# A hybrid decoder layer on one core: seven products for eight in some chunk pairs of the feed-forward streams, and eight PSUM banks as two alternating sets

## The chip, the cores and the metric

One core of a Trainium2 chip runs the whole layer. The metric is device time in microseconds (us) of one execution; lower is better. Before the change the median of three runs is 1110.67 us (1109.77 to 1110.89).

## The reference

The input is a sequence of 256 tokens by 2048 features, float32. After a normalisation and a combined input projection, two groups of attention heads run (latent attention and differential attention); their outputs are concatenated and go through one output projection `w_o`, which is added to the input. What the change touches is the feed-forward part behind it:

```
h = rmsnorm(x, ffn_norm)
x = x + (silu(h @ w_gate) * (h @ w_up)) @ w_down
```

`w_gate` and `w_up` are 2048 x 5632, `w_down` is 5632 x 2048. All of it is float32, and the result is compared as such.

## The kernel before, in words

**Streams.** Every projection is a *stream* (`stream`, L111): a weight matrix of up to 1024 columns is read from memory in order and used once, against both halves of the tokens. The contraction is cut into chunks of 128 rows. One DMA on SP's queue brings two chunks (a *pair*, 1 MB) into a tile `raw`, of which there are three (L139 to L144). The attention takes the first third of the span; from 372 us on the feed-forward part runs as gate0, up0, gate1, up1, down00, down01 (part 0), the same with gate2, up2, gate3, up3, down10, down11 (part 1), and gate4, up4, gate5, up5, down20, down21 (part 2). Gate and up streams have 16 chunks, down streams 16 (parts 0 and 1) or 12 (part 2). gate5 and up5 have 512 columns, all others 1024.

**Three matmuls for one product.** The matmul format keeps fewer bits than float32, so each operand is split into a high piece and a low piece. For a chunk of weights ACT casts `whi` from `raw` (L149), and DVE subtracts it from `raw` to get `wlo` (L150). There are four buffers for each (pool `wsp`, L75). The activations are split once, into `hth` and `htl` for gate and up (`h_prep`, L846), and into `fh` and `fl` for down (`ff_T`, L901). A product of 128 tokens by 512 columns is then three matmuls: high by high (L128), high by low (L129), low by high (L132). A chunk has two halves of tokens and two blocks of 512 columns, so 12 matmuls, and a pair has 24.

**PSUM.** There are eight banks of 128 x 512: tags `acc` (4), `tr` (2, for transposes) and `sc` (2). A stream accumulates in four banks (`acc_tile`, L97; with `wide`, in `acc` and `sc` in turn). At its end `evac` empties them: `gate_evac` (L891) is a Silu on ACT, `up_evac` (L895) a multiplication on DVE, `down_evac` (L931) and `o_evac` (L835) additions into `x2` on DVE.

**Work beside the streams.** A stream takes a list `bg` of functions and calls them between its chunks. In gate1, gate3, gate5 and in the first down stream of each part these are the four `ff_T`: four transposes on PE (L905), a cast on ACT (L909), a subtraction on DVE (L910). In o1, the stream ahead of gate0, they are `h_prep(0)`; `h_prep(1)` follows behind o1.

**Order.** A planner in the compiler sets the order of each engine's queue from the program's order and its own plan of when operands and buffers are ready; each engine then works through its queue in that order. So what is written later in the program can stand earlier in a queue.

Of the kernel before, what the change touches and what calls it, by code (L numbers as in the profile page):

```python
# [9 lines left out]
F32 = mybir.dt.float32  # L10
F32R = mybir.dt.float32r
BF16 = mybir.dt.bfloat16
AF = mybir.ActivationFunctionType
ALU = mybir.AluOpType
# [54 lines left out]
def body(ctx, tc, a):  # L69
# [6 lines left out]
    outer = ctx.enter_context(tc.tile_pool(name="outer", bufs=1))  # L76
    wraw = ctx.enter_context(tc.tile_pool(name="wraw", bufs=3))
    small = ctx.enter_context(tc.tile_pool(name="small", bufs=4))
    ps = ctx.enter_context(tc.tile_pool(name="ps", bufs=1, space=bass.MemoryType.PSUM))

    G = const.tile([P, NG], F32, name="G")
    cst = const.tile([P, NCST], F32, name="cst")
# [11 lines left out]

    rot = [0]

    def acc_tile(wide):  # L97
        tag, n = "acc", 4
        if wide:
            if rot[0] % 6 >= 4:  # L100
                tag, n = "sc", 2
            rot[0] += 1
        return ps.tile([P, 512], F32, name="acc", tag=tag, bufs=n)

    def tr_tile():
        return ps.tile([P, 512], F32, name="tr", tag="tr", bufs=2)

    def sc_tile():
# [2 lines left out]
    def stream(name, lhs, evac, bg=(), wide=False, pre=None, by=None, defer=False, last=False):  # L111
# [49 lines left out]

        if last:
            return None

        def finish():
            for tt in range(NT):
                for b, (b0, bn) in enumerate(blocks):
                    evac(tt, b, b0, bn, acc[tt][b][:, :bn])

        if defer:  # L170
            return finish
        finish()

    def rstd_of(ss, n, r):

# [659 lines left out]
    def o_evac(n):  # L835
        def f(tt, b, b0, bn, acc):
            F, x2 = ffn["F"], ffn["x2"]
            sl = slice(n * 1024 + b0, n * 1024 + b0 + bn)
            dve.tensor_tensor(out=x2[:, tt, sl], in0=acc, in1=x2[:, tt, sl], op=ALU.add)
            junk = F.tile([P, 512], F32, name="junk")  # L840
            act.activation(out=junk, in_=x2[:, tt, sl], func=AF.Square, accum_out=ss2[:, tt, 2 * n + b : 2 * n + b + 1])

        return f
# [23 lines left out]
    F, x2 = ffn["F"], ffn["x2"]  # L867
    hth = [outer.tile([P, 8, S], F32R, name="hth0", tag="low0"), outer.tile([P, 8, S], F32R, name="hth1", tag="xth1")]
    htl = [outer.tile([P, 8, S], F32R, name="htl0", tag="low1"), outer.tile([P, 8, S], F32R, name="htl1", tag="xtl1")]
    stream("o1", o_lhs, o_evac(1), bg=h_prep(0), wide=True)  # L870
    ssf = small.tile([P, NT], F32, name="ssf", bufs=1)
    dve.tensor_reduce(out=ssf, in_=ss2, axis=AX.X, op=ALU.add)
    rf = rstd_of(ssf, D, rstd_tile("rf", [P, NT]))
# [9 lines left out]
    for part, gs in enumerate(FFN_PARTS):  # L883
        fh = [outer.tile([P, 8, S], F32R, name=f"fh{i}", tag=("Tckv", "Tcq")[i]) for i in range(2)]
        fl = [outer.tile([P, 8, S], F32R, name=f"fl{i}", tag=("xth0", "xtl0")[i]) for i in range(2)]
        at = 0
        bg = []
        for gi in gs:
            held = {}

            def gate_evac(tt, b, b0, bn, acc):  # L891
                t = held[tt, b] = F.tile([P, 512], F32, name="sg", bufs=6)
                act.activation(out=t, in_=acc, func=AF.Silu, scale=rf[:, tt : tt + 1])

            def up_evac(tt, b, b0, bn, acc):  # L895
                t = held[tt, b]
                dve.scalar_tensor_tensor(
                    out=t, in0=acc, scalar=rf[:, tt : tt + 1], in1=t, op0=ALU.mult, op1=ALU.mult
                )

            def ff_T(tt, b, t, c0):  # L901
                def f():
                    p = tr_tile()
                    for j in range(4):
                        pe.transpose(out=p[:, j * P : (j + 1) * P], in_=t[:, j * P : (j + 1) * P], identity=ident)  # L905
                    pv = p.rearrange("p (j s) -> p j s", j=4)
                    sl = slice(tt * P, (tt + 1) * P)
                    hi = fh[c0 // 8][:, c0 % 8 : c0 % 8 + 4, sl]
                    act.copy(out=hi, in_=pv)  # L909
                    dve.tensor_tensor(  # L910
                        out=fl[c0 // 8][:, c0 % 8 : c0 % 8 + 4, sl], in0=pv, in1=hi.bitcast(F32), op=ALU.subtract
                    )

                return f

            stream(f"gate{gi}", h_lhs, gate_evac, bg=bg, wide=True)
            stream(f"up{gi}", h_lhs, up_evac, wide=True)
            bg = [
                ff_T(tt, b, held[tt, b], at // P + 4 * b)
                for b in range(FFN_COLS[gi] // 512)  # L920
                for tt in range(NT)
            ]
            at += FFN_COLS[gi]

        def f_lhs(kc, tt):
            sl = slice(tt * P, (tt + 1) * P)
            return fh[kc // 8][:, kc % 8, sl], fl[kc // 8][:, kc % 8, sl]

        for n in range(2):

            def down_evac(tt, b, b0, bn, acc):  # L931
                sl = slice(n * 1024 + b0, n * 1024 + b0 + bn)
                dve.tensor_tensor(out=x2[:, tt, sl], in0=acc, in1=x2[:, tt, sl], op=ALU.add)
                if part == len(FFN_PARTS) - 1:
                    nc.sync.dma_start(out=out_v[:, tt, sl], in_=x2[:, tt, sl])

            stream(
                f"down{part}{n}", f_lhs, down_evac, bg=() if n else bg, by=8, wide=True,
                last=part == len(FFN_PARTS) - 1 and n == 1,
            )  # L940

# [106 lines left out]
```

## Time and profile before

| | |
|---|---|
| median of three runs | 1110.67 us |
| the profiled execution | 1110.09 us |
| its span, first to last instruction | 1108.3 us |
| PE (matmuls) busy | 1095.3 us, 99% |
| DVE busy | 624.8 us, 56% |
| ACT busy | 519.1 us, 47% |
| granted PE clock | full in every slice |
| moved by DMA | 206 MB, 186 GB/s on average |

PE runs matmuls, PEld their weight loads beside them, DVE is the vector engine, ACT the scalar engine, SP the queue that issues most DMAs. A group line of the profile gives line, engine, operation, tiles written and read, shape and count, then busy time and mean ns of one, and the idle time ahead of it with what ended it. A timeline line gives start, length, engine, line and operation, with the idle time before it in brackets. Matmuls overlap: two neighbours start about 0.227 us apart, though each is shown as 0.39 us long, so PE's pace is read from starts.

### The profile page before, as it was taken

To read this page: it belongs to the slowest core of one execution; us is meant where nothing else is said; L and a number is where in the kernel's file an instruction comes from. 1 tells how busy PE (TensorE), PEld (TensorE's weight loads), DVE (VectorE), ACT (ScalarE), POOL (GpSimd) and SP (SyncE) were. 2 spreads that over 40 slices of the span, in tenths; PEclk is the share of its full clock that TensorE was granted. 3 is DMA by queue.
4 is the path that set the end of the run, shared out by engine and by line. 5 is a ranking of instruction groups with operands and counts; after the bars stand their busy time and mean duration, and the time that the engine had idled before them with its cause. 6 is when DMAs were issued, how large, how long until landed. Compare 5 with 4: busy or idle time off the path is not lost.

```text
span 1108.3 us, 12977 instructions
## 1 busy us (share of the span) xinstructions
PE 1095.3 (99%) x5114; PEld 904.2 (82%) x5114; DVE 624.8 (56%) x898; ACT 519.1 (47%) x706; POOL 31.8 (3%) x22
## 2 busy tenths in 40 slices
PE   8999999999999999999999999999999999999998
PEld 7878887877888888888888888888888888888886
DVE  7588667689655644544555454454454554445553
ACT  6585464557444535344343334335343333435431
POOL 0021003110100000000000000000000000000000
PEclk9999999999999999999999999999999999999999
DMA  8845434443375455555555555554555555535761
GB/s 285 288 167 209 154 113 157 174 164 114 118 277 193 172 190 193 191 188 187 190 190 190 190 192 192 199 189 178 195 190 184 193 194 198 195 116 184 256 222 75
DMA packets 37358, 206.37 MB, mean 186 GB/s; under 512 B 3633, under 2 KB 4017, under 8 KB 15281
## 3 DMA queue, kind: packets, MB, share of 16 engines
q1 hardware_dynamic: 36192, 200.82, 51.6%
q10 hardware_dynamic: 1104, 4.72, 1.2%
q8 instruction: 40, 0.66, 0.2%
q14 instruction: 22, 0.17, 0.0%
HBM read 203.43 MB, written 2.10 MB: 185 GB/s over the span
## 4 chain that ended last, share of the span: by engine, by line
PE 87%; DVE 6%; DMA 2%; ACT 2%; POOL 1%; issue 1%; ACTq 0%; DVEq 0%; POOLq 0%
PE acc L129 28%; PE acc L128 28%; PE acc L132 28%; DVE wlo L150 3%; PE sc L590 1%; PE tr L905 1%; ACT whi L149 1%; PE tr L481 1%; DMA raw<-in_w_kup 1%; DMA raw<-in_w_down 1%; DMA G<-in_G 1%; ACT p L621 1%; POOL rdq L181 1%; DVE p L604 0%; POOL rk L181 0%
## 5 line engine op out<-in xcount | busy, mean ns | idle before, releaser
L150 DVE TENSOR_TENSOR wlo<-raw,whi 128x1024 fp32r<-128x1024 f32 (+2 forms) x408 | 462.3, 1137 | 421.1 <-ACT whi L149 420.7
L149 ACT CAST whi<-raw 128x1024 fp32r<-128x1024 f32 (+2 forms) x408 | 400.0, 983 | 522.8 <-PE acc L132 493.7
L128 PE MATMUL acc<-whi,hth 128*128 128x512 f32 x704 | 275.5, 391 | 0.0
L129 PE MATMUL acc<-wlo,hth 128*128 128x512 f32 x704 | 274.3, 390 | 0.0
L132 PE MATMUL acc<-whi,htl 128*128 128x512 f32 x704 | 222.8, 390 | 0.0
L132 PEld LDWEIGHTS acc<-whi,htl 128*128 128x128 f32 x704 | 132.2, 188 | 27.6
L129 PEld LDWEIGHTS acc<-wlo,hth 128*128 128x128 f32 x704 | 132.3, 188 | 27.0
L128 PEld LDWEIGHTS acc<-whi,hth 128*128 128x128 f32 x704 | 132.3, 188 | 27.0
L128 PE MATMUL acc<-whi,fh 128*128 128x512 f32 x352 | 138.2, 393 | 0.0
L129 PE MATMUL acc<-wlo,fh 128*128 128x512 f32 x352 | 137.3, 390 | 0.4 <-DVE wlo L150 0.4
L128 PE MATMUL acc<-whi,xth 128*128 128x512 f32 (+1 forms) x288 | 108.6, 384 | 0.9 <-ACT whi L149 0.9
L132 PE MATMUL acc<-whi,fl 128*128 128x512 f32 x352 | 109.2, 390 | 0.0
L129 PE MATMUL acc<-wlo,xth 128*128 128x512 f32 (+1 forms) x288 | 105.5, 372 | 1.0 <-DVE wlo L150 1.0
L132 PE MATMUL acc<-whi,xtl 128*128 128x512 f32 (+1 forms) x288 | 85.8, 370 | 0.0
L129 PEld LDWEIGHTS acc<-wlo,fh 128*128 128x128 f32 x352 | 66.2, 188 | 14.2 <-DVE wlo L150 0.9
L132 PEld LDWEIGHTS acc<-whi,fl 128*128 128x128 f32 x352 | 66.0, 188 | 14.0 <-DVE fl L910 0.2
L128 PEld LDWEIGHTS acc<-whi,fh 128*128 128x128 f32 x352 | 66.1, 188 | 13.6 <-ACT fh L909 0.2
L128 PEld LDWEIGHTS acc<-whi,xth 128*128 128x128 f32 x288 | 53.8, 188 | 11.0 <-ACT whi L149 2.0
L129 PEld LDWEIGHTS acc<-wlo,xth 128*128 128x128 f32 x288 | 54.0, 188 | 9.1 <-DVE wlo L150 1.7
L132 PEld LDWEIGHTS acc<-whi,xtl 128*128 128x128 f32 x288 | 52.3, 188 | 9.3
L128 PE MATMUL acc<-whi,othm 128*128 128x512 f32 x64 | 26.5, 414 | 1.1 <-DVE dvn L200 1.1
L128 PE MATMUL acc<-whi,othd 128*128 128x512 f32 x64 | 25.2, 394 | 0.0
(252 smaller groups left out, 774.7 us busy)
## 6 DMA issues: line engine op xcount, KB each, us to landing
raw<-in_w_down SPq DMA_DIRECT2D x44, 1024.0 KB, 4.8
raw<-in_w_gate SPq DMA_DIRECT2D x40, 1024.0 KB, 4.8
raw<-in_w_up SPq DMA_DIRECT2D x40, 1024.0 KB, 4.8
raw<-in_w_o SPq DMA_DIRECT2D x16, 1024.0 KB, 4.9
raw<-in_w_dq SPq DMA_DIRECT2D x8, 1024.0 KB, 4.9
raw<-in_w_dk SPq DMA_DIRECT2D x8, 1024.0 KB, 4.8
raw<-in_w_dv SPq DMA_DIRECT2D x8, 1024.0 KB, 4.8
raw<-in_w_cq SPq DMA_DIRECT2D x8, 512.0 KB, 4.7
```

What stands on the lines that cost most here:

```text
L128: pe.matmul(o, lhsT=xh, rhs=hi[:, b0 : b0 + bn], start=kc == 0, stop=False)
L129: pe.matmul(o, lhsT=xh, rhs=lo[:, b0 : b0 + bn], start=False, stop=False)
L132: pe.matmul(o, lhsT=xl, rhs=hi[:, b0 : b0 + bn], start=False, stop=kc == nkc - 1)
L149: act.copy(out=hi[:, :cols], in_=raw[:, j, :cols])
L150: dve.tensor_tensor(out=lo[:, :cols], in0=raw[:, j, :cols], in1=hi[:, :cols].bitcast(F32), op=ALU.subtract)
L181: pool.tensor_tensor(out=r, in0=ss, in1=e.to_broadcast(shape), op=ALU.pow)
L481: pe.transpose(out=t[:, j, tt * P : (tt + 1) * P], in_=x[:, tt, hh * P : (hh + 1) * P], identity=ident)
L590: pe.matmul(t[:, P * qb : P * (2 * qb + 1)], lhsT=qt[:, qb * P : (qb + 1) * P], rhs=kt[:, : P * (qb + 1)], start=i == 0 and qb == 1, stop= ...
L621: act.activation(out=out[:, sl], in_=out[:, sl], func=AF.Exp, bias=b[:, qb : qb + 1], scale=scale[qb], accum_out=total[qb])
L905: pe.transpose(out=p[:, j * P : (j + 1) * P], in_=t[:, j * P : (j + 1) * P], identity=ident)
```

## The change

**Seven products.** `stream7` replaces `stream` in gate0 to gate4, up0 to up4, down00, down01, down10, down11 and down20. A pair of chunks, two halves of tokens and two blocks of columns make a 2 x 2 by 2 x 2 block product. In the pairs named in `sums` (2, 4 and 6 of the eight pairs of a gate or up stream; 1 and 3 of a down stream) it is computed from seven block products of three matmuls, not eight. For that, sums and differences of the four weight blocks are made for each such pair on DVE (`T`, its two halves once more, in `seven`) and split as the weights are (`cut`), and sums of the activation blocks once for each group of streams (`sums7`: three for `hth`, two for `fh` in each part). The other pairs run as before, as `eight`.

**Sharing.** Products 2, 3, 4 and 8 accumulate in four banks through the whole stream, products 1, 5, 6, 7 in four others through the seven-product pairs alone. Behind the last such pair these four are combined (`u`: one copy on ACT, four additions on DVE), and at the end `evac` adds `u` to the four accumulators; in down streams `u` is added to `x2` early.

**Banks.** From o1 on the three PSUM tags are replaced by a new pool of eight banks in two sets. A stream accumulates in one set; transposes and products 1, 5, 6, 7 use the other; after each stream the sets change places. `sg` has four buffers, not six.

```diff
@@ -76,7 +76,8 @@
...
     small = ctx.enter_context(tc.tile_pool(name="small", bufs=4))
-    ps = ctx.enter_context(tc.tile_pool(name="ps", bufs=1, space=bass.MemoryType.PSUM))
+    psA = ExitStack()
+    ps = psA.enter_context(tc.tile_pool(name="ps", bufs=1, space=bass.MemoryType.PSUM))
...
@@ -94,7 +95,22 @@
     rot = [0]
+    banks = {"at": 1, "acc": 0, "free": 0}
+    def bank(kind):
+        own = banks["at"] if kind == "acc" else 1 - banks["at"]
+        i = 4 * own + banks[kind] % 4
+        banks[kind] += 1
+        return banks["ps"].tile([P, 512], F32, name="acc" if kind == "acc" else "tr", tag=f"p{i}")
+    def change_over():
+        banks["at"] ^= 1
+        banks["acc"] = banks["free"] = 0
     def acc_tile(wide):
+        if "ps" in banks:
+            return bank("acc")
...
     def tr_tile():
+        if "ps" in banks:
+            return bank("free")
         return ps.tile([P, 512], F32, name="tr", tag="tr", bufs=2)
@@ -161,6 +179,8 @@
         if last:
             return None
+        if "ps" in banks:
+            change_over()
...
+    def stream7(name, lhs, order, sums, evac, bg=(), by=2, early=None):
...
+        final = [t for t in order if t in sums][-1]
+        lasts = {i: order[-1] if i in (2, 3, 4, 8) else final for i in range(1, 9)}
+        p = {}
...
+        def product(i, t, parts):
+            first = i not in p
+            if first:
+                p[i] = bank("acc" if i in (2, 3, 4, 8) else "free")
+            n = 3 * len(parts)
+            k = 0
+            for xh, xl, wh, wl in parts:
+                for x, w in ((xh, wh), (xh, wl), (xl, wh)):
+                    k += 1
+                    pe.matmul(p[i], lhsT=x, rhs=w, start=first and k == 1, stop=t == lasts[i] and k == n)
+        def cut(hi, lo, in_):
+            act.copy(out=hi, in_=in_)
+            dve.tensor_tensor(out=lo, in0=in_, in1=hi.bitcast(F32), op=ALU.subtract)
+        def pieces():
+            return [wsp.tile([P, 1024], F32R, name=n) for n in ("whi", "wlo")]
+        def seven(t, raw):
+            th = [F.tile([P, 1024], F32R, name=f"th{i}") for i in range(2)]
+            tl = [F.tile([P, 1024], F32R, name=f"tl{i}") for i in range(2)]
+            b1, b2 = pieces(), pieces()
+            T = F.tile([P, 1024], F32, name="T")
+            dve.tensor_tensor(
+                out=T.rearrange("p (i f) -> p i f", i=2),
+                in0=raw[:, :, 512:],
+                in1=raw[:, 0].rearrange("p (i f) -> p i f", i=2),
+                op=ALU.subtract,
+            )
+            cut(b1[0][:, :512], b1[1][:, :512], raw[:, 0, :512])
+            cut(*b2, raw[:, 1])
+            cut(th[0], tl[0], T)
+            dve.tensor_tensor(out=T[:, :512], in0=raw[:, 1, 512:], in1=T[:, :512], op=ALU.subtract)
+            dve.tensor_tensor(out=T[:, 512:], in0=raw[:, 1, :512], in1=T[:, :512], op=ALU.subtract)
+            cut(th[1], tl[1], T)
...
+            for i, x, w in (
+                (1, lhs(k1, 0), of(b1, 0)),
+                (2, lhs(k2, 0), of(b2, 0)),
+                (3, S[3], of(b2, 1)),
+                (5, S[0], of((th[0], tl[0]), 0)),
+                (7, S[2], of((th[0], tl[0]), 1)),
+                (6, S[1], of((th[1], tl[1]), 0)),
+                (4, lhs(k2, 1), of((th[1], tl[1]), 1)),
+            ):
+                product(i, t, [(*x, *w)])
+                if i in (2, 5, 7, 4):
+                    background()
+        def eight(t, raw):
+            w = []
+            for j in range(2):
+                w.append(pieces())
+                cut(*w[j], raw[:, j])
+            def part(i, j):
+                tt, half = {2: (0, 0), 3: (0, 1), 4: (1, 0), 8: (1, 1)}[i]
+                return (*lhs(2 * t + j, tt), *(v[:, 512 * half : 512 * half + 512] for v in w[j]))
+            if t != order[-1]:
+                for j in range(2):
+                    for i in (2, 3, 4, 8):
+                        product(i, t, [part(i, j)])
+                        if i in (3, 8):
+                            background()
+            else:
+                for i in (2, 3, 4, 8):
+                    product(i, t, [part(i, j) for j in range(2)])
+                    background()
+        u = {}
+        for t in order:
+            raw = wraw.tile([P, 2, 1024], F32, name="raw")
+            nc.sync.dma_start(out=raw, in_=src[t].rearrange("p (j f) -> p j f", j=2))
+            if t in sums:
+                seven(t, raw)
+            else:
+                eight(t, raw)
+            if t == final:
+                u = {i: F.tile([P, 512], F32, name="ev", bufs=6) for i in (2, 3, 4, 8)}
+                act.copy(out=u[2], in_=p[1])
+                for o, b, x in ((3, 6, 2), (4, 7, 3), (8, 5, 4), (3, 5, 3)):
+                    dve.tensor_tensor(out=u[o], in0=p[b], in1=u[x], op=ALU.add)
+                for i, tt, b in ((2, 0, 0), (4, 1, 0), (8, 1, 1), (3, 0, 1)) if early else ():
+                    early(tt, b, u[i])
+        change_over()
+        for i, tt, b in ((2, 0, 0), (3, 0, 1), (4, 1, 0), (8, 1, 1)):
+            evac(tt, b, p[i], u[i])
+    def sums7(name, hi, lo):
+        F = ffn["F"]
+        parts = [F.tile([P, 4, P], F32R, name=name + x) for x in "hl"]
+        def f():
+            h = F.tile([P, 2, S], F32, name="h", tag="ev", bufs=6)
+            c = F.tile([P, 4, P], F32, name="hc", tag="ev", bufs=6)
+            dve.tensor_tensor(out=h, in0=hi.bitcast(F32), in1=lo.bitcast(F32), op=ALU.add)
+            a11, a12, a21, a22 = h[:, 0, :P], h[:, 1, :P], h[:, 0, P:], h[:, 1, P:]
+            for o, in0, in1, op in (
+                (0, a21, a22, ALU.add), (2, a11, a21, ALU.subtract),
+                (1, c[:, 0], a11, ALU.subtract), (3, a12, c[:, 1], ALU.subtract),
+            ):
+                dve.tensor_tensor(out=c[:, o], in0=in0, in1=in1, op=op)
+            act.copy(out=parts[0], in_=c)
+            dve.tensor_tensor(out=parts[1], in0=c, in1=parts[0].bitcast(F32), op=ALU.subtract)
+        return parts, f
...
@@ -837,7 +1000,7 @@
             F, x2 = ffn["F"], ffn["x2"]
             sl = slice(n * 1024 + b0, n * 1024 + b0 + bn)
             dve.tensor_tensor(out=x2[:, tt, sl], in0=acc, in1=x2[:, tt, sl], op=ALU.add)
-            junk = F.tile([P, 512], F32, name="junk")
+            junk = F.tile([P, 512], F32, name="junk", tag="ev", bufs=6)
             act.activation(out=junk, in_=x2[:, tt, sl], func=AF.Square, accum_out=ss2[:, tt, 2 * n + b : 2 * n + b + 1])
         return f
@@ -867,7 +1030,15 @@
     F, x2 = ffn["F"], ffn["x2"]
     hth = [outer.tile([P, 8, S], F32R, name="hth0", tag="low0"), outer.tile([P, 8, S], F32R, name="hth1", tag="xth1")]
     htl = [outer.tile([P, 8, S], F32R, name="htl0", tag="low1"), outer.tile([P, 8, S], F32R, name="htl1", tag="xtl1")]
-    stream("o1", o_lhs, o_evac(1), bg=h_prep(0), wide=True)
+    h_sums, f_sums, make_h = {}, {}, []
+    for t in (2, 4, 6):
+        sl = slice(2 * t % 8, 2 * t % 8 + 2)
+        h_sums[t], f = sums7(f"h{t}", hth[t // 4][:, sl], htl[t // 4][:, sl])
+        make_h.append(f)
+    psA.close()
+    banks["ps"] = ctx.enter_context(tc.tile_pool(name="ps8", bufs=1, space=bass.MemoryType.PSUM))
+    stream("o1", o_lhs, o_evac(1), bg=[*h_prep(0), make_h[0]], wide=True)
     ssf = small.tile([P, NT], F32, name="ssf", bufs=1)
     dve.tensor_reduce(out=ssf, in_=ss2, axis=AX.X, op=ALU.add)
     rf = rstd_of(ssf, D, rstd_tile("rf", [P, NT]))
@@ -884,12 +1055,12 @@
         fh = [outer.tile([P, 8, S], F32R, name=f"fh{i}", tag=("Tckv", "Tcq")[i]) for i in range(2)]
         fl = [outer.tile([P, 8, S], F32R, name=f"fl{i}", tag=("xth0", "xtl0")[i]) for i in range(2)]
         at = 0
-        bg = []
+        bg, make_f = [] if part else make_h[1:], []
         for gi in gs:
             held = {}
             def gate_evac(tt, b, b0, bn, acc):
-                t = held[tt, b] = F.tile([P, 512], F32, name="sg", bufs=6)
+                t = held[tt, b] = F.tile([P, 512], F32, name="sg", bufs=4)
                 act.activation(out=t, in_=acc, func=AF.Silu, scale=rf[:, tt : tt + 1])
             def up_evac(tt, b, b0, bn, acc):
@@ -913,8 +1084,27 @@
                 return f
-            stream(f"gate{gi}", h_lhs, gate_evac, bg=bg, wide=True)
-            stream(f"up{gi}", h_lhs, up_evac, wide=True)
+            def gate_add(tt, b, acc, u):
+                t = held[tt, b] = F.tile([P, 512], F32, name="sg", bufs=4)
+                dve.tensor_tensor(out=t, in0=acc, in1=u, op=ALU.add)
+                act.activation(out=t, in_=t, func=AF.Silu, scale=rf[:, tt : tt + 1])
+            def up_add(tt, b, acc, u):
+                dve.tensor_tensor(out=u, in0=acc, in1=u, op=ALU.add)
+                up_evac(tt, b, 0, 0, u)
+            if FFN_COLS[gi] == 1024:
+                stream7(f"gate{gi}", h_lhs, range(8), h_sums, gate_add, bg=bg)
+                stream7(f"up{gi}", h_lhs, range(8), h_sums, up_add, bg=make_f, by=8)
+                make_f = []
+            else:
+                stream(f"gate{gi}", h_lhs, gate_evac, bg=bg, wide=True)
+                stream(f"up{gi}", h_lhs, up_evac, bg=make_f, wide=True)
+                make_f = []
+            if gi == gs[0]:
+                for t in (1, 3):
+                    f_sums[t], f = sums7(f"f{t}", fh[0][:, 2 * t : 2 * t + 2], fl[0][:, 2 * t : 2 * t + 2])
+                    make_f.append(f)
             bg = [
                 ff_T(tt, b, held[tt, b], at // P + 4 * b)
                 for b in range(FFN_COLS[gi] // 512)
@@ -934,10 +1124,18 @@
                 if part == len(FFN_PARTS) - 1:
                     nc.sync.dma_start(out=out_v[:, tt, sl], in_=x2[:, tt, sl])
-            stream(
-                f"down{part}{n}", f_lhs, down_evac, bg=() if n else bg, by=8, wide=True,
-                last=part == len(FFN_PARTS) - 1 and n == 1,
-            )
+            def down_early(tt, b, u):
+                sl = slice(n * 1024 + 512 * b, n * 1024 + 512 * b + 512)
+                dve.tensor_tensor(out=x2[:, tt, sl], in0=u, in1=x2[:, tt, sl], op=ALU.add)
+            def down_add(tt, b, acc, u):
+                down_evac(tt, b, 512 * b, 512, acc)
+            if part == len(FFN_PARTS) - 1 and n == 1:
+                stream(f"down{part}{n}", f_lhs, down_evac, last=True)
+            else:
+                order = [0, 2, 1, 4, 3, 5, 6, 7][: GROUPS[f"down{part}{n}"][0] // 256]
+                stream7(f"down{part}{n}", f_lhs, order, f_sums, down_add, bg=() if n else bg, early=down_early)
```

## Rows read from the trace of the kernel before

**Rows 1.** The page: span; part 1: engines, busy time, share, instructions.

```profile
span 1108.3 us, 12977 instructions
...
PE 1095.3 (99%) x5114; PEld 904.2 (82%) x5114; DVE 624.8 (56%) x898; ACT 519.1 (47%) x706; POOL 31.8 (3%) x22
```

**Rows 2.** Stretches: length; busy PE, PEld, DVE, ACT, POOL (instructions); clock; DMA, GB/s.

```profile
372.15:1080.00 707.85, 707.42 (x3168) 585.03 (x3167) 359.60 (x350) 303.01 (x335) 0.69 (x1) 1.00 0.55 191
...
620.00:663.52 43.52, 43.52 (x193) 36.05 (x192) 21.91 (x21) 16.88 (x16) 0.00 (x0) 1.00 0.55 194
```

**Rows 3.** Timeline of SP's queue: the weight loads of gate2, up2 and gate3.

```profile
620.05 38.41 SPq L144 DMA_DIRECT2D raw<-in_w_gate  x8
663.57 38.41 SPq L144 DMA_DIRECT2D raw<-in_w_up  x8
707.09 38.91 SPq L144 DMA_DIRECT2D raw<-in_w_gate  x8
```

**Rows 4.** Groups by shape from 372.15 us to the end.

```profile
L150 DVE TENSOR_TENSOR wlo<-raw,whi 128x1024 fp32r<-128x1024 f32 x245 | 299.7, 1225 | 329.5 <-ACT whi L149 329.5
...
L149 ACT CAST whi<-raw 128x1024 fp32r<-128x1024 f32 x245 | 258.1, 1055 | 386.6 <-PE acc L132 383.1 <-DMA raw<-in_w_down 3.6
...
L150 DVE TENSOR_TENSOR wlo<-raw,whi 128x512 fp32r<-128x512 f32 x32 | 22.1, 691 | 21.7 <-ACT whi L149 21.7
...
L933 DVE TENSOR_TENSOR x<-acc,x 128x512 f32<-128x512 f32 x24 | 15.2, 683 | 6.5 <-PE acc L132 6.5
...
L897 DVE SCALAR_TENSOR_TENSOR sg<-acc,rf,sg 128x512 f32<-128x512 f32 x22 | 15.0, 742 | 0.0
...
L905 PE MATMUL tr<-cst,sg 128*128 128x128 f32 x88 | 13.2, 273 | 0.0
...
L205 DVE SCALAR_TENSOR_TENSOR htl<-tr,G,hth 128x256 fp32r<-128x256 f32 x10 | 4.5, 480 | 0.1
```

**Rows 5.** Timeline of PE's last chunk, one bank after the other.

```profile
1099.29 0.39 PE L128 MATMUL acc<-whi,fh 128*128 128x512 f32 x1
...
1099.97 0.39 PE L128 MATMUL acc<-whi,fh 128*128 128x512 f32 x1
```

**Rows 6.** Timeline: neighbours on DVE; a cast on ACT with its subtraction.

```profile
338.81 1.22 DVE L150 TENSOR_TENSOR wlo<-raw,whi 128x1024 fp32r<-128x1024 f32 x1 [1.50 <-ACT whi L149]
339.95 0.48 DVE L205 SCALAR_TENSOR_TENSOR htl<-tr,G,hth 128x256 fp32r<-128x256 f32 x1
...
559.09 1.05 ACT L149 CAST whi<-raw 128x1024 fp32r<-128x1024 f32 x1 [1.68 <-PE acc L132]
560.18 1.22 DVE L150 TENSOR_TENSOR wlo<-raw,whi 128x1024 fp32r<-128x1024 f32 x1 [1.39 <-ACT whi L149]
...
595.46 2.48 DVE L933 TENSOR_TENSOR x<-acc,x 128x512 f32<-128x512 f32 x4
```

**Rows 7.** Timeline of DVE and PE where up1 ends and down00 begins.

```profile
548.80 1.23 DVE L150 TENSOR_TENSOR wlo<-raw,whi 128x1024 fp32r<-128x1024 f32 x1 [1.50 <-ACT whi L149]
...
549.94 2.72 DVE L897 SCALAR_TENSOR_TENSOR sg<-acc,rf,sg 128x512 f32<-128x512 f32 x4
...
550.46 0.39 PE L129 MATMUL acc<-wlo,fh 128*128 128x512 f32 x1
...
552.58 1.22 DVE L150 TENSOR_TENSOR wlo<-raw,whi 128x1024 fp32r<-128x1024 f32 x1
```

**Rows 8.** Start of gate0: a stretch as in rows 2, two timeline rows.

```profile
372.15:385.03 12.88, 12.88 (x66) 10.61 (x65) 11.05 (x19) 10.20 (x22) 0.69 (x1) 1.00 0.47 156
...
383.60 1.23 DVE L150 TENSOR_TENSOR wlo<-raw,whi 128x1024 fp32r<-128x1024 f32 x1 [0.74 <-ACT whi L149]
...
385.03 0.39 PE L128 MATMUL acc<-whi,hth 128*128 128x512 f32 x1
```

**Rows 9.** Timeline where o0 ends and o1 begins.

```profile
326.21 2.48 DVE L839 TENSOR_TENSOR x<-acc,x 128x512 f32<-128x512 f32 x4
...
326.96 0.49 PE L128 MATMUL acc<-whi,othm 128*128 128x512 f32 x1
```

More of the change, by code (lines that the diff above doesn't have):

```diff
@@ L172, in stream, with background, of @@
         finish()
+    def stream7(name, lhs, order, sums, evac, bg=(), by=2, early=None):
+        src = a["w_" + name].rearrange("(t p) f -> t p f", p=P)
+        F = ffn["F"]
+        bg = list(bg)
+        done = [0, 0]
+        final = [t for t in order if t in sums][-1]
+        lasts = {i: order[-1] if i in (2, 3, 4, 8) else final for i in range(1, 9)}
+        assert order[0] not in sums and order[-1] not in sums
+        p = {}
+        def background():
+            done[1] += 1
+            while done[0] < min(len(bg), len(bg) * done[1] // (4 * by)):
+                bg[done[0]]()
+                done[0] += 1
+        def product(i, t, parts):
[30 more added lines that the diff above has]
+            cut(th[1], tl[1], T)
+            S = [(sums[t][0][:, i], sums[t][1][:, i]) for i in range(4)]
+            k1, k2 = 2 * t, 2 * t + 1
+            def of(ops, half):
+                return tuple(x[:, 512 * half : 512 * half + 512] for x in ops)
+            for i, x, w in (
[43 more added lines that the diff above has]
+                    early(tt, b, u[i])
+        assert done[0] == len(bg)
+        change_over()
+        for i, tt, b in ((2, 0, 0), (3, 0, 1), (4, 1, 0), (8, 1, 1)):
+            evac(tt, b, p[i], u[i])
@@ new lines, in sums7 @@
+    def sums7(name, hi, lo):
+        F = ffn["F"]
+        parts = [F.tile([P, 4, P], F32R, name=name + x) for x in "hl"]
[12 more added lines that the diff above has]
+        return parts, f
```

## The prediction, made before the changed kernel was run

> **What bounds the kernel now.** I read the page's busy shares first: PE is at 99%, DVE at 56%, ACT at 47% [rows 1]. A busy PE need not be at its pace, so I read stretches and starts next. In the feed-forward part PE is idle 0.43 us of 707.85, at the full clock (2.4 GHz), with 3168 matmuls, nearly all 512 columns wide [rows 2]. Two whole streams, gate2 and up2, lie between the first loads of gate2 and gate3: 87.04 us [rows 3]. That is 2 x 192 matmuls, so 0.2267 us for one, with nothing lost at the stream's end. DMA is at 0.55 there [rows 2]. DVE works 21.9 us of a 43.5 us stream [rows 2], and the groups say what stops it: the subtraction waits for the cast, and the cast for PE to give a buffer back (383 us of idle time in front of L149, ended by L132) [rows 4]. So PE sets the time, DVE and ACT run as far ahead as four buffers allow, and a matmul taken out is worth 0.2267 us as long as they keep up.
>
> **What goes.** A pair takes 24 matmuls, a seven-product pair 21. Ten gate and up streams have three such pairs, five down streams two: 30 x 3 + 10 x 3 = 120 matmuls, 120 x 0.2267 = **27.2 us**. Three matmuls in a row now go into one bank; the last chunk of the kernel does this already, at (1099.97 - 1099.29) / 3 = 0.227 us each [rows 5], so the new order costs nothing. Every matmul keeps its weight load. The transposes stay 88 [rows 4]. They move from the whole of a gate stream to its first two pairs; the first is then due 12 matmuls, 2.7 us, into the stream and stands in PE's queue, so it waits for `up_add` and `up_evac` of the stream ahead. The last pair of a stream finishes one bank after another, the first 4.1 us before the end, so two 0.7 us steps on DVE are in time if DVE is.
>
> **What DVE gets.** An ordinary pair costs DVE two subtractions of 1024 columns. A seven-product pair costs four of 1024 (`T`, the low pieces of block row 2, of `th0` and `th1`) and three of 512 (the low piece of one block and the two new halves of `T`). One alone takes 1.225 us, and 0.691 at 512 columns [rows 4]. Where the next one need not wait it starts earlier: 1.14 us behind the start of a 1024 one, and four 512 additions end after 2.48 us, so (2.48 - 0.683) / 3 = 0.60 apart [rows 4, 6]. A seven-product pair is then 4 x 1.14 + 3 x 0.60 = 6.4 us, and one wait lies in it that cannot be packed: the second half of `T`, the cast of `th1`, its low piece. That is 0.69 + 0.04 + 1.055 + 0.04 (the hand-over in rows 6) in place of 0.60: 1.2 us more.
>
> One gate and one up stream: ten ordinary pairs 22.8, six seven-product pairs 38.2, their waits 7.3, two chains of four additions for `u` (three depend on each other) 5.5, eight additions of `u` 4.8, four `up_evac` at (2.72 - 0.742) / 3 = 0.66 [rows 4, 7] 2.6. **81.2 us on DVE, against 2 x 183 x 0.2267 = 83.0 on PE.** A down stream: 13.7 + 12.7 + 2.4 + 2.8 + eight additions 4.8 = 36.4, with four `ff_T` 38.8, against 186 x 0.2267 = 42.2. So DVE goes from half idle to full, and still fits. ACT gets four casts (0.5 + 3 of 1024) where it had two: about 25 us a stream, covered by PE.
>
> **Whether it fits in place.** `th` and `T` have one buffer each, so a seven-product pair can be prepared only once PE is through the last one. In the unstalled plan the fifth product of such a pair frees `th0` at 3.4 of its 4.8 us, an ordinary pair of 5.4 follows, and the sixth product of the next one needs the low piece of `th1` at 3.4: 1.4 + 5.4 + 3.4 = 10.2 us later. In that time DVE has what follows the cast of `th0` (6.4 + 1.2 less the 2.9 of `T` and the first two low pieces, 4.7) and the ordinary pair's 2.3. That leaves some 3 us of lead, enough for one burst at a stream's end (four steps of 0.60 or 0.66). It is enough only if DVE's queue holds the work in the order in which it is due. Today's queue does: the subtraction at 548.80, used by down00 from 550.46 on, stands ahead of up1's four multiplications at 549.94 [rows 7].
>
> Terms that the trace does not show directly:
> - *Start of gate0.* PE reaches pair 2 at 385.03 and needs its last low piece 3.6 us on, at 388.6, which is 16.5 us after gate0 began. DVE's 11.05 us of the first 12.88 hold three subtractions for pair 2 and later (one at 383.60), leaving 7.4 [rows 8]. To these come three `sums7`, each two 512 steps and four 128-column ones of at most 0.48 (nearest: 256 columns [rows 4]), so 1.4 to 3.3, say 2.6, and pair 2's 8.2 at full durations: 23.4 in all. Nearly 7 us late; but two of the sums are due only for pairs 4 and 6, and neighbours pack. Between 0 and 7 I take **4**.
> - *Start of down00 and down10.* One `sums7` and the transposes' casts fall on the burst: 0 to 2.6 each, I take 1, so **2**.
> - *New PSUM pool at o1.* Half the old `acc` banks may lie in o1's set. Today PE loses 0.1 us there, beside a 2.48 us row of evacuations [rows 9]. Between 0 and 2.6 I take **1**, since o1 can begin with the banks that were free.
> - *Each of the 15 ends.* `u` and its copies, late by up to one 0.60 us step; below, nothing. As DVE has spare time, 0.2 each: **3**.
>
> The profiled execution took 1110.09 us, 0.58 below the median: 1110.1 - 27.2 + 4 + 2 + 1 + 3 = 1089.9. **I predict 1090 us.** All unknown costs at nothing give 1083, all at their upper ends (7 + 5 + 3 + 9) 1107.
>
> **Rival 1: DVE becomes the pace.** If neighbours do not pack, the durations of rows 4 count in full. One gate and one up stream are then 24.5 + 41.8 + 6.8 + 5.7 + 5.5 + 3.0 = 87.3 us on DVE, and PE's 83.0 no longer matter: nothing is gained on the 87.04 of today. Down streams, at 39 to 42, still gain 6 x 0.2267 each, 6.8 in all. With the first three terms above, 1110.1 - 6.8 + 1.5 + 0 to 7 gives **1105 to 1112**. Half-way, packed only where operands are long ready, it is 1098. For it: most subtractions will follow a cast that ended just before. Against it: rows 6, where neighbours do pack. The Trainium skill bears on this ("VectorE: DVE Perf Modes", section "The DRAIN you can't avoid"): there a next operation starts only when the pipe of the last one is empty. By that rule the time would be this rival's. The trace disagrees, with a start 1.14 us behind one that lasts 1.22, so I give it less than even weight.
>
> **Rival 2, slower: the combining blocks the last pair.** It is one place. The four additions for `u` are written ahead of the last pair's subtractions and wait for product 6 of the last seven-product pair. If DVE's queue keeps that order, the last pair's low piece comes 3 x 0.72 + 0.68 + 1.225 + 0.08 = 4.1 us behind product 6, while PE has 0.91 us of work left (product 4 and one matmul); the second low piece adds 0.5. A stall of 3.7 us in each of 15 streams is 55 us: 1110.1 - 27.2 + 55 = 1138, with the other terms **1138 to 1145**. It decides from 27.2 / 15 = 1.8 us a stream on, or 1.35 with those terms. For it: the order of the program. Against it: rows 7, where DVE's queue takes later work first. By the Trainium skill ("TensorE: Matmul & The Clock Gate", section "Architectural detail: the array is 16× 32×32, not 1× 128×128") ACT and DVE are strict first-in first-out, so a wrong plan would not mend itself; no row here shows either.
>
> **Rival 3: the matmuls stay.** If the count of PE's instructions does not fall by 120 from 5114 [rows 1], nothing is gained and the added terms cost 3 to 10 us. I see no way for it in the diff and put it inside the slower chance.
>
> **Chances.** Forecast 0.67, rival 1 0.18, rivals 2 and 3 0.15. A measurement here can tell about 0.2%, 2.2 us. Rival 1 splits into 0.11 faster and 0.07 the same; so faster 0.78, same 0.07, slower 0.15. For 8 in 10 the range starts at the bare gain, 1082, and goes through most of rival 1, to 1108; rival 2 stays out.
>
> **What would show it.** In the profile after: 4994 PE matmuls; seven-product pairs 4.76 us apart on PE; gate to gate 83 us plus little; DVE near 95% in gate and up streams. DVE's neighbouring subtractions 1.14 apart speak for the forecast, 1.27 for rival 1. Additions of `u` ahead of the last pair's subtractions, with PE waiting for L150's successor, would be rival 2. The forecast is wrong if PE's idle time in the feed-forward part passes 15 us.

## The result, and the profile after

| | before | after |
|---|---|---|
| median | 1110.78 us (4 runs) | 1093.51 us (4 runs, 1091.69 to 1095.45) |
| ratio, 95% interval | | 0.9845 [0.9825, 0.9865] |
| the profiled execution, span | 1110.09, 1108.3 | 1091.69, 1089.9 |
| PE matmuls | 5114 | 4994 |
| DVE, ACT busy | 56%, 47% | 80%, 54% |

The kernel is faster by 17.3 us, where 20.7 were forecast and 27.2 is the worth of the matmuls taken out. First the page after, the span and part 1, against [rows 1]:

```profile
span 1089.9 us, 13272 instructions
...
PE 1076.0 (99%) x4994; PEld 884.5 (81%) x4994; DVE 877.0 (80%) x1272; ACT 585.4 (54%) x810; POOL 31.8 (3%) x22
```

The 120 matmuls are gone. DVE has 252 us more work, and PE is as busy as before. Next the stretches, with the columns of [rows 2]: the feed-forward part but for its last stream; gate2 and up2 by PE, from gate2's first matmul to gate3's; gate1 and up1 in the same way; then the time from gate2's first load to up2's and from there to gate3's.

```profile
378.38:1056.00 677.62, 677.62 (x3020) 556.50 (x3020) 603.52 (x713) 364.98 (x433) 0.69 (x1) 1.00 0.55 197
...
636.00:719.32 83.32, 83.32 (x368) 68.72 (x366) 73.22 (x79) 45.24 (x51) 0.00 (x0) 1.00 0.57 208
463.58:549.00 85.42, 85.42 (x384) 70.21 (x382) 79.82 (x95) 47.77 (x56) 0.00 (x0) 1.00 0.55 197
...
617.45:660.11 42.66, 42.66 (x190) 35.22 (x189) 36.02 (x40) 19.86 (x22) 0.00 (x0) 1.00 0.55 197
660.11:701.76 41.65, 41.65 (x184) 34.35 (x183) 36.83 (x40) 23.89 (x28) 0.00 (x0) 1.00 0.55 202
```

PE has no idle time in 677 us. Gate2 and up2 take PE 83.3 us against 87.04 [rows 3], so 3.7 of the 4.1 us that their 18 matmuls are worth came. The forecast of "gate to gate 83 us plus little" holds. DVE is busy for 73.2 of the 83.3 us, 88%; in gate1 and up1, where the work on `ff_T` comes on top, for 79.8 of 85.4, 93%. (Between the loads lie 42.66 + 41.65 = 84.3 us with 72.9 of DVE. The loads of a stream start when buffers come free, so they aren't PE's pace; some of the expectations below go by them.)

So most of the loss lies elsewhere. I cut both traces at two matmuls that have the same work on either side, the last of o0 and the first of gate0, and read their starts (and that of the kernel's last matmul) from PE's timeline:

| stretch of PE | before | after | difference |
|---|---|---|---|
| start to the last matmul of o0 | 326.28 | 327.95 | +1.7 |
| from there to the first of gate0 (o1) | 45.95 | 49.75 | +3.8 |
| from there to the kernel's last matmul | 731.6 | 707.7 | -23.9 |

The sum is the 18.4 us between the two profiled executions. The feed-forward part gives 23.9 of 27.2; o1, where no matmul changed, gives 3.8 back. The timeline where o0 ends and o1 begins, first PE's before, beside the evacuations of [rows 9]:

```profile
326.05 0.61 PE L132 MATMUL acc<-whi,otld 128*128 128x512 f32 x2
326.51 0.39 PE L128 MATMUL acc<-whi,othm 128*128 128x512 f32 x1
```

Then PE's and DVE's after:

```profile
327.73 0.61 PE L150 MATMUL acc<-whi,otld 128*128 128x512 f32 x2
327.88 2.48 DVE L1002 TENSOR_TENSOR x<-acc,x 128x512 f32<-128x512 f32 x4
...
330.51 0.60 PE L146 MATMUL acc<-whi,othm 128*128 128x512 f32 x1 [2.17 <-DVE x L1002]
...
330.91 0.63 PE L147 MATMUL acc<-wlo,othm 128*128 128x512 f32 x1
...
333.90 0.49 PE L146 MATMUL acc<-whi,othm 128*128 128x512 f32 x1
334.23 0.39 PE L147 MATMUL acc<-wlo,othm 128*128 128x512 f32 x1
```

o1's first matmul waits until the *fourth* of o0's evacuations has ended, 327.88 + 2.48 = 330.36. PE stands still: 330.51 - 327.95 = 2.56 us from start to start, where 0.23 is usual. Behind the stop the matmuls start 0.40 to 0.43 us apart, until 333.9, and the stretch shows why:

```profile
330.00:340.00 10.00, 9.49 (x35) 7.73 (x36) 3.75 (x4) 3.99 (x9) 0.00 (x0) 0.83 0.30 105
```

The granted clock is 0.83 on average here: for a third of the stretch it is at its lower level, 1.2 in place of 2.4 GHz. The eight matmuls from 330.51 to 333.90 take 3.39 us where eight steps of 0.227 are 1.81, so 1.6 us. The stop costs 2.56 - 0.23 = 2.3, and the two together are the 3.8 us but for 0.1. The Trainium skill ("TensorE: Matmul & The Clock Gate", section "What's actually happening") says that the lower clock is the default and that activity releases it; a fall behind a stop agrees with that.

### The profile page after: what moved, and what is told of

Its sections match the earlier page's. It is cut to its first block, busy times and chain, and to the rows that moved or that the text cites. A ratio compares the mean times of both kernels' runs of the same rounds, so it can differ in the third digit from the quotient of the medians.

```text
span 1089.9 us, 13272 instructions
## 1 busy us (share of the span) xinstructions
PE 1076.0 (99%) x4994; PEld 884.5 (81%) x4994; DVE 877.0 (80%) x1272; ACT 585.4 (54%) x810; POOL 31.8 (3%) x22
## 4 chain that ended last, share of the span: by engine, by line
PE 88%; DVE 5%; DMA 2%; ACT 2%; POOL 2%; issue 1%; SPq 0%; ACTq 0%; DVEq 0%; POOLq 0%
PE acc L228 47%; PE tr L228 10%; PE acc L146 9%; PE acc L147 9%; PE acc L150 9%; DVE wlo L168 2%; PE sc L753 1%; PE tr L1076 1%; PE tr L644 1%; DMA raw<-in_w_ckv 1%; DMA raw<-in_w_kup 1%; DMA raw<-in_w_cq 1%; ACT p L784 1%; POOL rdq L344 1%; ACT whi L167 1%
## 5 line engine op out<-in xcount | busy, mean ns | idle before, releaser
L231 ACT CAST whi<-raw 128x512 fp32r<-128x512 f32 (+1 forms) x236 | 225.7, 978 | 185.5 <-PE acc L228 163.3
L232 DVE TENSOR_TENSOR wlo<-raw,whi 128x512 fp32r<-128x512 f32 (+1 forms) x236 | 261.5, 1132 | 34.1 <-ACT whi L231 33.2
L168 DVE TENSOR_TENSOR wlo<-raw,whi 128x1024 fp32r<-128x1024 f32 (+2 forms) x172 | 173.2, 1018 | 89.1 <-ACT whi L167 88.4
L167 ACT CAST whi<-raw 128x1024 fp32r<-128x1024 f32 (+2 forms) x172 | 150.9, 884 | 153.0 <-PE acc L150 116.4
L228 PE MATMUL acc<-whi,hth 128*128 128x512 f32 x430 | 168.3, 391 | 0.0
L228 PE MATMUL acc<-wlo,hth 128*128 128x512 f32 x430 | 167.7, 390 | 0.0
L228 PE MATMUL acc<-whi,htl 128*128 128x512 f32 x430 | 167.6, 390 | 0.0
L231 ACT CAST th<-T 128x1024 fp32r<-128x1024 f32 x80 | 84.1, 1051 | 81.2 <-DVE T L253 40.0
L232 DVE TENSOR_TENSOR tl<-T,th 128x1024 fp32r<-128x1024 f32 x80 | 97.8, 1223 | 22.6 <-ACT th L231 21.1
L228 PEld LDWEIGHTS acc<-wlo,hth 128*128 128x128 f32 x430 | 80.8, 188 | 17.1
```

Source lines behind the costliest of these rows:

```text
L167: act.copy(out=hi[:, :cols], in_=raw[:, j, :cols])
L168: dve.tensor_tensor(out=lo[:, :cols], in0=raw[:, j, :cols], in1=hi[:, :cols].bitcast(F32), op=ALU.subtract)
L228: pe.matmul(p[i], lhsT=x, rhs=w, start=first and k == 1, stop=t == lasts[i] and k == n)
L231: act.copy(out=hi, in_=in_)
L232: dve.tensor_tensor(out=lo, in0=in_, in1=hi.bitcast(F32), op=ALU.subtract)
```

## The experiments

Each kernel is the changed one with one edit. The kernel before ran beside each group: medians 1109.5, 1110.09 and 1109.87 us. "Stretch" is the time from the first matmul of gate0 to the last of the kernel, as in the table above.

**The sets alone.** All streams go through `stream` and no sums of activations are made; pool and sets stay.

```diff
...
-            if FFN_COLS[gi] == 1024:
+            if False:
...
-            if part == len(FFN_PARTS) - 1 and n == 1:
+            if True:
```

> The new pool and the two alternating sets alone; every stream has all its eight-product pairs, no sums are made. 5114 matmuls. Theory A: slower than the kernel before by the stop at o1 and its half clock, 2 to 4 us, so 1112.5 to 1115; streams of 43.52 us as before. Theory C (the sets bring something of their own, or cost at every change of place): each of the 17 changes shows, and the time moves by more than 5 us either way.

1113.8 us, ratio 1.004 [1.0024, 1.0055]: 4.3 us slower than before. o1 takes 49.86 us, so the stop is there; the stretch takes 731.8, as before the change. The alternating sets cost and bring nothing that shows; o1, with the change-over of pools, takes 3.9 us more than before and so has nearly all of the 4.3.

**Seven products in gate and up alone, and in down alone.** The same two edits, one at a time.

> Seven products in the ten gate and up streams alone; the down streams have all their eight-product pairs, in the two sets. 90 matmuls less than the kernel before, 20.4 us. Theory A (PE sets the pace; the pool's stop costs 3.8): against sets alone (4.3 us slower than the kernel before) 18 to 20.5 us faster, so 14 to 16 us faster than the kernel before. Theory B (DVE is the pace of gate and up): these streams give little, 0 to 8 us.

> Seven products in the five down streams alone. 30 matmuls less, 6.8 us. Theory A: 6 to 7 us faster than sets alone, so 2 to 3 us faster than the kernel before. Theory B: the same here, as DVE fits in down streams by both. So this run and the one with gate and up alone should add up to what the whole change gives beyond the sets, 25 us by the last call (4.3 + 20.9).

| seven products in | matmuls out | worth | stretch | gained | ratio to the kernel before |
|---|---|---|---|---|---|
| nothing (sets alone) | 0 | 0 | 731.8 | | 1.004 [1.0024, 1.0055] |
| down | 30 | 6.8 | 724.6 | 7.2 | 0.9984 [0.9968, 0.9999] |
| gate and up | 90 | 20.4 | 714.0 | 17.8 | 0.9868 [0.9844, 0.9893] |
| both | 120 | 27.2 | 707.7 | 24.1 | 0.9845 [0.9825, 0.9865] |

Gains add up: 7.2 + 17.8 = 25.0 against 24.1. These stretches are one execution each, and the changed kernel's own differ by up to 1.4 us (707.3 to 708.7 in three), so 7.2 for a worth of 6.8 means no more than all of it. Gate and up still give 87% of their worth. By theory B they would have given 8 us at most; it falls. (The medians: 1108.61 and 1096.57 us. Gate and up alone came out 13.5 us faster than the kernel before, a little under the 14 to 16 expected; down alone 1.5, under the 2 to 3.)

**No new pool.** The sets are made of the old tags, `acc` (4) as one, `tr` and `sc` (2 + 2) as the other.

```diff
-        return banks["ps"].tile([P, 512], F32, name="acc" if kind == "acc" else "tr", tag=f"p{i}")
+        tag, n = ("acc", 4) if own == 0 else ("tr", 2) if i % 4 < 2 else ("sc", 2)
+        return ps.tile([P, 512], F32, name="acc" if kind == "acc" else "tr", tag=tag, bufs=n)
...
-    psA.close()
-    banks["ps"] = ctx.enter_context(tc.tile_pool(name="ps8", bufs=1, space=bass.MemoryType.PSUM))
+    banks["ps"] = ps
```

> The changed kernel without its new PSUM pool: the two sets are the old tags (acc as one set; tr and sc as the other), so o1 starts in the four banks that o0 does not use. Theory A (PE sets the pace everywhere; of the 8.8 us lost against 27.2, 2.1 are PE's stop between o0 and o1 and 1.7 the half clock behind it): PE's stop between o0 and o1 goes, the clock stays full there, and the time falls by 3 to 4 us, to 1089 to 1090.5. Theory B (DVE is the pace of the gate and up streams, and PE's stop at o1 is only filled time): DVE's work is as before and the time stays within 1 us of 1093.5.

> The changed kernel once more, as the control on the chip of the other runs. Both theories: 1091.5 to 1095.5 us, with PE's stop of 2.1 us between o0 and o1 again. Theory A adds that the drop of the clock at 185 us, behind the 2.6 us stop that both kernels have in the attention part, is chance: it may be missing here or stand in the kernel before.

The timeline of the same place in the version without the new pool:

```profile
324.09 0.62 PE L150 MATMUL acc<-whi,otld 128*128 128x512 f32 x2
324.25 2.48 DVE L1002 TENSOR_TENSOR x<-acc,x 128x512 f32<-128x512 f32 x4
324.55 0.39 PE L146 MATMUL acc<-whi,othm 128*128 128x512 f32 x1
```

And its busy times and clock between 330 and 340 us:

```profile
330.00:340.00 10.00, 10.00 (x47) 8.26 (x46) 5.10 (x7) 5.10 (x6) 0.00 (x0) 1.00 0.57 194
```

o1 starts 0.23 us behind o0, beside the evacuations, in the banks that o0 doesn't use; the clock stays at 1.00. o1 takes 45.75 us, 4.0 less. The median is 1086.0 us, ratio 0.9789 [0.9768, 0.9809], against 1088.61 and 0.9814 [0.9796, 0.9832] for the changed kernel beside it. That is 2.6 us, under the 3 to 4 expected. Both medians are lower than expected (1089 to 1090.5, and 1091.5 to 1095.5), so both kernels ran once more.

> The changed kernel without the new pool, a second time, beside the changed kernel on the same chip. If the stop at o1 and the half clock behind it cost 3.8 us of PE's time (theory A), it is 3 to 4 us faster than the changed kernel again; if the 2.6 us of the last call were spread between runs, the two are within 1 us.

> The changed kernel once more, for the run beside it: 17 to 21 us faster than the kernel before.

1088.44 us, 0.9796 [0.9783, 0.981], against 1089.87, 0.9816 [0.9802, 0.9829]: 1.4 us, which is neither the 3 to 4 of one expectation nor the "within 1 us" of the other. The traces are as clear as at first: o1 takes 45.75 us here and 49.80 there. So the 4.0 us in o1 are shown by five traces, and 1.4 to 2.6 of them by the medians. What can blur the medians is the rest of the span: in the five profiled executions of these two kernels the part ahead of o1, which no edit touches, took 324.3 to 328.4 us, and the stretch behind o1 707.3 to 708.9. Part of the first spread arises at one place. All profiled kernels, the one before too, have a stop of PE in the attention part, near 182 us, of some 2.85 us from start to start; behind it the clock fell in six of twelve executions, with the new pool and without, and stayed up in the others, the kernel before among them. This version is the fastest of the study, 23.5 and 21.4 us under the kernel before by the two pairs of medians.

**More work on DVE.** Two subtractions of 512 columns more in each seven-product pair, then six; their results are not used.

```diff
+            X = F.tile([P, 512], F32, name="X", tag="ev", bufs=6)
+            for _ in range(2):
+                dve.tensor_tensor(out=X, in0=raw[:, 0, :512], in1=raw[:, 1, :512], op=ALU.subtract)
```

> The changed kernel with two more 512-column subtractions on DVE in each seven-product pair (results unused): 1.2 us each, 40 pairs, 48 us more work on DVE, 7.2 in a gate and up stream together. By the sum of the prediction (81.2 us on DVE against 83.0 on PE) 5.4 us of each of the five gate and up streams would show: 25 us slower, near 1119. Theory A with the measured busy time of 72.9 us in 84.3 (the waits are filled with other work): the 7.2 fit, the time rises by 0 to 6 us, to 1093 to 1100. Theory B: all 36 us of the gate and up streams show, near 1129.

> Six more 512-column subtractions on DVE in each seven-product pair, 3.6 us each, 21.6 in a gate and up stream together. Measured room there is 11.4 us (72.9 busy in 84.3), so by theory A extended by the last call DVE must now be the pace: at least 10 us over in each of five gate and up streams, 50 to 75 us slower than the changed kernel, 1140 to 1165. If the time rises only in line with the run of two subtractions (9.6 us for 48 us of work, so about 29), the room is larger than the busy time says.

With two, 1098.26 us, ratio 0.99 [0.988, 0.992], which is 9.7 us over the changed kernel beside it (1088.61) where 0 to 6 were expected; the stretch is 7.9 us longer, for 48 us of work. With six, 1174.96 us, 1.0576 [1.0547, 1.0606]; the stretch is 81.6 us longer, for 144. Busy times between 390 and 1050 us in the kernel with two, then in the kernel with six, and there once more where the clock was lowest:

```profile
390.00:1050.00 660.00, 655.74 (x2900) 534.73 (x2899) 616.13 (x748) 349.81 (x404) 0.00 (x0) 1.00 0.54 195
```

```profile
390.00:1050.00 660.00, 613.77 (x2591) 481.45 (x2589) 644.04 (x818) 310.55 (x350) 0.00 (x0) 0.98 0.47 172
...
574.00:588.00 14.00, 10.47 (x33) 7.64 (x34) 14.00 (x22) 4.79 (x7) 0.00 (x0) 0.63 0.48 163
```

And two of the waits with six, from 378 us on (us in total, times, the longest):

```profile
ACT th L231 <- DVE T L243: 98.2, 33, 5.8
...
PEld tr L228 <- ACT th L231: 28.6, 23, 2.1
```

DVE goes from 89% (603.52 of 677.62 in the changed kernel) to 93% and to 98%. At 98% it is the pace: ACT waits for DVE's sums, PE for ACT's casts. At 89% PE is. The edge is gradual: at 93% PE already loses 4 us of 660. By PE's starts 5.1 of the 7.9 us stand in down00 and down10, behind the ends of up streams, and 1.5 in gate1 and up1. By the room that I worked out beforehand, 1.8 us in a gate and up stream, two more would have cost 25 us. DVE's idle time tells better where the loss stands: in gate2 and up2 it is 83.3 - 73.2 = 10.1 us, and 7.2 more cost nothing there (83.3 us again); in gate1 and up1 it is 85.4 - 79.8 = 5.6, and 7.2 more cost the 1.5. The rule is a rough one: gate3 and up3 have the same 5.6 and lose 0.5. With six the rise is more than I expected (50 to 75). I hadn't counted the clock: PE now stops often, and in five spells, 23.9 us of the stretch, the granted clock is at its lower level. 38 matmuls start 0.38 to 0.46 us apart in them, 7.6 us more than at the usual pace; as DVE sets the pace there, how much of that adds to the 81.6 isn't known.

**The combining first.** A small addition that reads `u` and writes into the last pair's low pieces, overwritten by the subtraction behind it. It forces DVE's order of rival 2.

```diff
+                if t == order[-1]:
+                    dve.tensor_tensor(out=w[j][1][:, :64], in0=u[3][:, :64], in1=u[8][:, :64], op=ALU.add)
```

> The changed kernel with the order of the second rival forced: a 64-column addition of u into the low pieces of a stream's last pair, overwritten by the subtraction behind it, so that DVE's queue must do the combining ahead of the last pair's subtractions. In the gate and up streams and in down20 the last seven-product pair is next to last, 11 streams. By the rival's price of 3.7 us each: 41 us slower than the changed kernel, near 1130. If the planner can move other products in front on PE (as it does at the start of gate0), less: 0 to 20 us.

The end of gate2 in this kernel, DVE and PE, then two stretches, all from gate0 on and the one with the lowest clock:

```profile
683.61 2.74 DVE L311 TENSOR_TENSOR ev<-tr,ev 128x512 f32<-128x512 f32 x4 [4.78 <-PE tr L228]
...
684.05 1.79 PE L228 MATMUL acc<-whi,hth 128*128 128x512 f32 x7
686.39 0.36 DVE L280 TENSOR_TENSOR wlo<-ev 128x64 fp32r<-128x64 f32 x2
686.41 0.50 PE L228 MATMUL acc<-whi,hth 128*128 128x512 f32 x1 [0.57 <-DVE ev L311]
686.66 3.49 DVE L232 TENSOR_TENSOR wlo<-raw,whi 128x1024 fp32r<-128x1024 f32 x3
...
687.94 0.50 PE L228 MATMUL acc<-wlo,hth 128*128 128x512 f32 x1 [1.03 <-DVE wlo L232]
```

```profile
374.79:1124.09 749.30, 725.41 (x3153) 585.17 (x3151) 620.97 (x755) 373.77 (x440) 0.69 (x1) 0.99 0.51 183
...
776.00:788.00 12.00, 9.46 (x27) 6.86 (x27) 9.75 (x14) 2.60 (x4) 0.00 (x0) 0.72 0.29 100
```

DVE is idle 4.78 us, then combines, then makes the low pieces, and PE stops twice. The planner moves seven matmuls forward (684.05) and still 1134.91 us come out, ratio 1.0221 [1.0192, 1.0251]. The stretch grows from 707.7 to 749.3: 41.6 us, against 11 x 3.7 = 41. That the two agree so well is luck. By PE's starts the eleven streams lose 2.1 to 6.8 us each, gate2 2.2, and part of it is the clock: for 17.1 us of the stretch, in four spells, it is at its lower level, and 33 matmuls start some 0.43 us apart in them, 6.6 us more than at the usual pace. That leaves 35 us to the stops, 3.2 a stream. Either way the whole gain, and more, hangs on this order.

## Why the prediction was right

The forecast was 1090 us in a range of 1082 to 1108; 1093.5 came. Its mechanism holds, but several of its terms were mis-sized, and its sum was added up wrongly: 1110.1 - 27.2 + 4 + 2 + 1 + 3 is 1092.9, not 1089.9. That 1092.9 lies so near the 1091.7 of the profiled execution is partly luck. Of the 9 us put down for the feed-forward part 3.3 came, of the 1 us at o1 3.8, and 1.7 came ahead of o1, where nothing was put down: 8.8 in place of 10.

**The matmuls.** 120 out, at 0.2267 each. With seven products in a row PE never waits long, but more matmuls start a few ns late. At the end of gate2 in the changed kernel:

```profile
670.17 2.36 DVE L232 TENSOR_TENSOR wlo<-raw,whi 128x1024 fp32r<-128x1024 f32 x2 [0.20 <-ACT whi L231]
...
671.96 0.40 PE L228 MATMUL acc<-th,htl 128*128 128x512 f32 x1
672.20 0.40 PE L228 MATMUL acc<-whi,hth 128*128 128x512 f32 x1
...
672.45 1.41 DVE L309 TENSOR_TENSOR ev<-tr,ev 128x512 f32<-128x512 f32 x2
...
673.78 0.69 DVE L1089 TENSOR_TENSOR sg<-acc,ev 128x512 f32<-128x512 f32 x1
```

The step from 671.96 to 672.20 is 0.24. Of the steps behind a 512-column matmul from gate0 on, 215 of 3167 were 0.229 to 0.26 before, together 1.5 us over 0.2267; now it is 738 of 3047 and 4.5 us. The cause is open. It is not that a matmul has to wait for a fresh piece or bank: 592 of the 738 carry no wait for a semaphore, and neither do their weight loads. These 3.0 us are most of what the stretch lacks (27.2 - 23.9 = 3.3). I had put 3 us down for the stream ends. That the sizes nearly agree is luck, as the place and the kind are others: no stop of PE in the stretch exceeds 0.2 us.

**DVE.** The work was sized well: 81.2 - 7.3 of waits = 73.9 us in a gate and up stream, measured 73.2 in gate2 and up2. Neighbours do pack, as [rows 6] said:

```profile
655.46 1.23 DVE L232 TENSOR_TENSOR tl<-T,th 128x1024 fp32r<-128x1024 f32 x1 [1.20 <-ACT th L231]
656.60 1.22 DVE L232 TENSOR_TENSOR wlo<-raw,whi 128x1024 fp32r<-128x1024 f32 x1
657.73 1.22 DVE L243 TENSOR_TENSOR T<-raw 128x1024 f32<-128x1024 f32 x1
658.87 2.96 DVE L232 TENSOR_TENSOR wlo<-raw,whi 128x1024 fp32r<-128x1024 f32 x3
```

Starts are 1.13 to 1.14 apart at 1.22 long. So rival 1 did not come. By the rule of the Trainium skill that the prediction cited ("VectorE: DVE Perf Modes", section "The DRAIN you can't avoid"), the next operation starts only when the pipe is empty. The same section of the Trainium skill adds that an operation that isn't held starts earlier, and it is this exception that the trace shows. The wait that I held to be unpackable, 1.20 us at 655.46, was packed in 26 of 40 pairs. The waits of the changed kernel from 350 us on, with the same columns, list 20 for the two low pieces `tl` of the 40 pairs, and 14 of these stand before a pair's second piece and are 1.2 us long:

```profile
DVE tl L232 <- ACT th L231: 21.1, 20, 1.2
```

That is in part why the sum of 81.2 against 83.0 was too strict, as the run with two more subtractions shows it to be.

**Start of gate0: 4 us were put down, 0.4 came.** From the first matmul of gate0 to 395 us PE lost 1.9 us to transposes and late starts, as before (1.9 in the first 17.3 us). Over the whole stream gate0 takes 2.3 us more than gate2, before 1.9. The term assumed that PE works through the products in the program's order. The planner put products of the next pair among those of pair 2:

```profile
395.30 0.49 PE L228 MATMUL tr<-th,h2h 128*128 128x512 f32 x1
395.63 0.39 PE L228 MATMUL acc<-th,hth 128*128 128x512 f32 x1
395.86 0.39 PE L228 MATMUL acc<-whi,hth 128*128 128x512 f32 x1
...
397.25 0.40 PE L228 MATMUL tr<-tl,h2h 128*128 128x512 f32 x1
```

Products with `th` stand apart from those with its low piece `tl`, and ordinary matmuls on `whi` fill the two us between. Of the 2 us for down00 and down10 0.9 came at most: they take 2.4 us more than down01 and down11, before 2.0, with no stop.

**The new pool: 1 us was put down, 3.8 to 4.0 came.** This is the step that failed. I took it that o1 could start in the banks that were free. The first matmul in the new pool waited for the last evacuation out of the old one, and the clock's fall behind the stop was in no term. Whether it waited for the old pool as a whole, or for one bank of it that was emptied last, no run separates.

**Part ahead of o1: 1.7 us** between the two profiled executions, by the spread described above. Without it and with 1 us at o1, the sum 1110.1 - 27.2 + 3.3 + 1 would have given 1087, and the version without the new pool comes to 1086.0 and 1088.4.

**Rival 2** had the price for a stream about right (3.7 us; 3.2 without the clock) and the wrong number of them: in the four longer down streams three pairs follow the last seven-product pair, so it is 11, not 15. It did not come because DVE's queue took the last pair's subtractions (670.17) ahead of the combining (672.45). Rival 3 fell with the count of 4994.

## What to carry to other kernels

Where one engine is full, work traded away from it is worth its own pace, one step for each instruction; the engine that takes the work over sets the limit, and its room is its idle time in that stage, here between 5.6 and 10.1 us in a pair of streams, less what bursts take, not the sum of a chain worked through in program order. Check that late combining does not stand in front of early preparation in an in-order queue: here that order alone made 41.6 us, some 6.6 of them in spells of the lower clock. Changing PSUM pools in the middle of a busy stretch made the first matmul wait here for the last evacuation out of the old pool; giving the old buffers new roles did not.

## What the runs showed of the hardware that was not expected

A stop of PE of 2.56 us from start to start at o1 was followed by the lower clock in each of the nine profiled executions that had it, and cost 1.6 to 1.7 us more; a longer one near 182 us, 2.85, was followed by it in six of twelve. Why one is always followed by it and the other not stays open. 523 more matmuls start some 6 ns late (3.0 us in all), most of them without a semaphore to wait for. On DVE a 1024-column instruction whose operands are ready starts 0.08 us before the last one's end.
